# Where the first four gated tiles of an output projection are fetched and split, and where a shift state is transposed

## The chip, the cores and the metric

The kernel runs on one core of a Trainium2 chip. The time is the device time of one execution in microseconds; the median of three runs before the change is 1459.28 us (1458.47 to 1459.82). The engines are named as the profile names them: PE (matrix products), PEld (its weight loads), DVE (elementwise), ACT (activations, copies, casts), POOL (elementwise), and SP, which in this kernel issues the DMAs.

## What is computed

A trunk of two layers over 544 tokens (512 of a prompt and 32 of a sample), 1024 wide. Layer 0 mixes tokens with a recurrence (RWKV-7, 24 heads of 64), layer 1 with differential attention. Each layer also has a cross-attention over a memory of 256 rows with four heads. Both results are multiplied by a gate and go through one output projection:

```python
def rwkv_layer(x, mk, mv, prev_row, S0, norm_w, w_out, w_in, ...):
    h = rmsnorm(x, norm_w)
    p, qm, gate = jnp.split(h @ w_in, [RW_PROJ, RW_PROJ + MEM_W], axis=-1)
    y_mix, S_T, last_row = rwkv_mixer(p, prev_row, S0, ...)
    y_mem = mem_attention(qm, mk, mv)
    out = jnp.concatenate([y_mix, y_mem], axis=-1) * jax.nn.silu(gate)
    return x + out @ w_out, S_T, last_row
```

`S_T` (the recurrence's state) and `last_row` (the last projected row, "shift state", 37 x 128 values for the prompt and as many for the sample) are outputs too. Products of float32 are made of three passes with operands split in a high and a low part: `hh`/`hl` of the activations, `whi`/`wlo` of the weights.

## The kernel before

**Tiling.** Channels lie on the 128 partitions and the 544 tokens along the free axis, taken in two halves of 272. A projection to 128 channels is 8 tiles of the contracted dimension, three passes (`hh,whi`, `hl,whi`, `hh,wlo`) and two halves: 48 matmuls of 128x272 into a `ps_g` bank. `wlo` is made on DVE from the raw weights and their cast `whi` (ACT).

**Layer 0.** The 24 heads are worked in 12 pairs, numbered 0 to 11. Inside a pair a chain of chunks runs hop by hop: a product into `ps_c`, an evacuation by DVE (`avz`, or the new state `SB`) or ACT (`sv`, `yt`, `sd`), the next product. Between the hops the projections of later pairs fill PE, taken from a generator (`main`). The sequence is written out by hand: `PLAN` has 23 rows k with two halves each, `MPLAN` puts the steps of the memory attention at (row, head) of the pairs 10 and 11. While `ordered` is set, every engine and SP's queue issue in the order in which the program emits: an instruction at the head of a queue that waits holds back all that is behind it. Weight subtractions and gatings are put off in a list, `later`, and `some(room)` emits as many as a budget of DVE time allows; `spent` counts what the budget has used. `until` forces what a block needs, just before the block starts.

**What is gated.** `put` sends a gated tile (128 channels x 544 tokens: 12 of the heads, 0 to 11, and 4 of the memory attention, 12 to 15) to DRAM scratch, `oscr`. For the output projection `fetch` brings it back into a tile `lo`, and `gated` splits it: `hi` is the cast, on ACT; `lo` becomes the rest by a subtraction, on DVE for even tiles and on POOL for odd ones (line 1161).

**The end of layer 0.** After pair 11 the gate of head pair 11 (called gate 11 here) is projected, and pair 11's outputs are finished by `rw_finish` ("fin", "rsq" in `TAIL`), ending with `yt`, five transposes `ps_y` and the last gating. Between these steps `fill2` takes matmuls, first of gate 11, then of the output projection. Its units (`w_out`) are a block k of 128 output channels, a half of the gated tiles, and four tiles of it; the first two units use tiles 0 to 3. `ahead` splits one fetched tile and fetches another; NGATED is how many are fetched in advance.

**Shift state.** At the end of pair 9 two 37x128 transposes (`ps_sh`), one copy (`sho`) and two DMAs put it out, ahead of the memory attention's first loads (`cmt`, `mhk`, `mhv`, `cmv`) in the program.

Of the kernel before, what the change touches and what calls it, by code (L numbers as in the profile page):

```python
# [9 lines left out]
F32 = mybir.dt.float32  # L10
# [7 lines left out]
P = 128  # L18
# [7 lines left out]
NPAIR = MIXW // P  # L26
NMEM = 256
MH = 4
RW_PROJ = 3 * MIXW + 128
NPROJ = RW_PROJ // P  # L30
# [7 lines left out]
RAWS = 5  # L38
SGB = 2
HNB = 3  # L40
NGATED = 4
MADE = 6


# [2 lines left out]
LATER = 0.75  # L47
# [23 lines left out]
    [[("prep", 3, 0, 1.45), ("val", 1, 0.45, 0)], [("prep", 3, 0, 0.5)]],  # L71
    [[("out", 0, 1.6, 0.7)], [("prep", 3, 0, 0)]]]
MEMPE = 4.8
MPLAN = {10: [(0, 0), (1, 0), (2, 0), (3, 0), (4, 0), (5, 0), (6, 0), (6.5, 1), (7, 0), (8, 0), (9, 0), (10, 0), (10.5, 0), (12.5, 1),
# [9 lines left out]
OUT_ORDER = [0, 1, 2, 3, 4, 5, 6, 7, 8, 9, 10, 12, 13, 14, 15, 11]  # L84
# [21 lines left out]
class Trunk:  # L106
# [758 lines left out]
    def rw_outputs(self, st):  # L865
# [7 lines left out]
        yield  # L873
        self.state_out(self.SB[pr % 2][0], self.o[2][0, 0, 2 * pr : 2 * pr + 2])

    def state_out(self, S, dst):
        nc, p = self.nc, self.rk0
        ps = self.psm.tile([P, 4, P], F32, tag="m", name="ps_so")
        self.te.transpose(ps[:, 0, :], S[:], self.ident[:])
        so = p.tile([P, 64], F32, tag="so", name="so", bufs=1)  # L880
        for h in range(2):
            hc = slice(64 * h, 64 * h + 64)
            self.ae.copy(so[hc, :], ps[hc, 0, hc])
        self.se.dma_start(dst.rearrange("h v k -> (h v) k"), so[:])
# [30 lines left out]
        return self.o1[g] if self.o1 else sg  # L915

    def put(self, g, t):
        if not self.o1:
            self.se.dma_start(self.oscr[g // 8][:, g % 8, :], t[:])

# [249 lines left out]
    def w_out(self, i, p, order, consume, extra=None, o=None):  # L1170


        came, o = [], o or {}
        left = [g for g in order if g not in o]

        def fetch():
            if left:
                g = left.pop(0)
                came.append((g, self.fetch(p, g)))

        def ahead(n):
            for _ in range(n):
                if came:
                    g, t = came.pop(0)
                    o[g] = self.gated(g, *t)
                    fetch()

        for _ in range(NGATED):
            fetch()
        half = [[g for g in order if g // 8 == q] for q in range(2)]  # L1190
        units = [(k, q, half[q][4 * j : 4 * j + 4], j == 1) for q in range(2) for j in range(2) for k in range(2)]
        units += [(k, q, half[q], True) for k in range(2, KT) for q in range(2)]
        ws, ps = {}, {}
        halves = [slice(0, TH), slice(TH, T)]

        def products():
            for k, q, gs, last in units:
                if (k, q) not in ws:
                    ws[k, q] = self.weights(None, 0)
                hi, lo = ws[k, q]  # L1200
                ahead(len([g for g in gs if g not in o]))
                if q == 0 and k not in ps:
                    pool, tag = (self.psc, "c") if k == 1 else (self.psg, "g")
                    ps[k] = [pool.tile([P, 512], F32, tag=tag, name="ps_g") for _ in range(2)]
                end = q == 1 and last
                for vs in [halves] if k < 2 else [[v] for v in halves]:
                    for j, g in enumerate(gs):
                        if k < 2 and (j + k) % 2 == 0:
                            ahead(1)
                        if end and extra is not None and j == len(gs) // 2:  # L1210
                            extra(k, vs)
                        for v in vs:
                            out = ps[k][v.start // TH][:, :TH]
                            wh, wl = hi[:, g % 8, :], lo[:, g % 8, :]
                            for x, y in ((wh, o[g][0]), (wh, o[g][1]), (wl, o[g][0])):
                                self.te.matmul(out, x, y[:, v], start=q == 0 and g == half[0][0] and x is wh and y is o[g][0],
                                                 stop=end and g == gs[-1] and x is wl)
                                yield
                    if vs[-1].stop == T and last:
                        self.used()  # L1220
                    if end:
                        for v in vs:
                            consume(k, ps[k][v.start // TH][:, :TH], v)

        return products(), ahead
# [29 lines left out]
    def layer0(self, mem):  # L1255
        nc, o = self.nc, self.o
# [4 lines left out]
        mctx, rctx = ExitStack(), self.rctx  # L1261
        with ExitStack() as ctx:
# [66 lines left out]
                        yield from self.mem_block(i, kind, h, *hl(), wt, out, self.psm, "m")  # L1329
                    add(None, src, h * P, make)  # L1330

            mems = [{} for _ in range(MH)]
            rw_gate = lambda pr, j: add_gate(pr, sts[j], RW_PROJ + 512 + j * P, j % 2)
            mem_gate = lambda pr, h: add_gate(pr, mems[h], RW_PROJ + 512 + MIXW + h * P, h // 2)
            add_mems(0, 1, lambda: mem)
# [91 lines left out]
            for pr in range(NPAIR):  # L1427
                mplan = MPLAN.get(pr, ())
                took = [HOP + sum(us for x in y for kind, d, us, _ in x if 0 <= pr + d < NPAIR) for y in PLAN]
                load = [HOPV[k % 3] + sum(us for x in y for kind, d, _, us in x if 0 <= pr + d < NPAIR) for k, y in enumerate(PLAN)]  # L1430
                whole = sum(took) + MEMPE * len(mplan) / 12 + MAIN * each[pr]

                pace = [max(x, 1.4) for x in load] if each[pr] < 3 * 6 * KT else [1.0] * len(PLAN)
                due = [whole * sum(pace[:k]) / sum(pace) for k in range(len(PLAN) + 1)]
                room = (sum(load) + 2.3 * each[pr] / 48) / len(PLAN)
                t, left, spent = 0.0, each[pr], 0.0
                for k, y in enumerate(PLAN):
                    go("chain", pr)
                    t += HOP
                    spent += HOPV[k % 3]  # L1440
                    for half, x in enumerate(y):
                        for kind, d, us, vus in x:
                            if 0 <= pr + d < NPAIR and kind != "full":
                                go(kind, pr + d)
                                t += us
                                spent += vus
                        for at, h in mplan:
                            if at == k + half / 2:
                                if h not in mit:
                                    mit[h] = self.mem_steps(mems[h], 0, h, self.ma)  # L1450
                                    next(mit[h])
                                next(mit[h], None)
                                t += MEMPE / 12
                        if FULL not in x:
                            spent += self.some(room * (k + (half + 1) / 2) + 0.4 - spent)
                        while left and t + MAIN / 2 < (due[k + 1] if half else (due[k] + due[k + 1]) / 2):
                            next(main)
                            t += MAIN
                            left -= 1
                while left:  # L1460
                    next(main)
                    left -= 1
                if pr + 3 == NPAIR:
                    for _ in range(3):
                        go("prep", pr + 2)
                    while self.later:
                        self.later.pop(0)[0]()
                    ca.close()
                    self.ma = self.pool("mem0a", 1, ctx=ma, side="right")
                    ps = self.psm.tile([P, 512], F32, tag="m", name="ps_sh")  # L1470
                    so = self.ma.tile([NPROJ, 2, P], F32, name="sho")
                    for q in range(2):
                        self.te.transpose(ps[:NPROJ, q * P : q * P + P], self.shc[:, q, :], self.ident[:])
                    self.ae.copy(so[:], ps[:NPROJ, :256].rearrange("p (q c) -> p q c", q=2))
                    for q, n in ((0, 3), (1, 9)):
                        self.se.dma_start(o[n][0, 0].rearrange("(j p) -> j p", p=P), so[:, q, :])

            go("out", NPAIR - 1)
            fill(6)
# [7 lines left out]
        with ExitStack() as ctx:  # L1487
            p = self.pool("wo0", 1, ctx=ctx)
# [31 lines left out]

            rows(0)
            self.ahead = after[2:] + [(self.a[n][1], h * P) for n in ("w_mem_k", "w_mem_v") for h in range(MH)] + self.blocks1()
            wout, ahead = self.w_out(0, p, OUT_ORDER, consume, residual)

            def both():
                yield from main
# [27 lines left out]
            for i in range(5):  # L1554
                n = P if i < 4 else TS
# [259 lines left out]
    def run(self):  # L1815
# [3 lines left out]
        self.psm = self.pool("psm", 2, space=PS)  # L1819
        self.psx = self.pool("psx", 1, space=PS)  # L1820
        self.psc = self.pool("psc", 2, space=PS)
        self.mem = {}
        self.ordered, self.later, self.open = False, [], []
        self.place_no = self.acted = 0
        nc = self.nc
# [61 lines left out]
```

## Time and profile before

| | |
|---|---|
| median of 3 runs | 1459.28 us |
| span of the profiled execution | 1461.1 us |
| PE busy in it | 1403.8 us (96%) |
| DVE, ACT, POOL busy | 63%, 57%, 29% |
| PE waits from 600 to 626 us (start of pair 10) | 2.2 for `cmt`, 1.2 for `sv`, 0.5 and 0.2 for `yt` |
| PE waits from 626 to 706 us (pairs 10 and 11) | 0.4 to 0.9 each, for `mp`, `yt`, `sg`, `so` |
| PE waits from 706 to 760 us (start of the output projection) | 1.6 for `yt`, 1.3 for `lo` of DVE, 0.9 for `hi`, 0.5 for `lo` of POOL |

The profiled execution's time is its span, first instruction to last; it lies 1.8 us above the median of the runs, which were not profiled. A row of the timeline is a start in us, a duration in us, engine, line, operation, and `out<-in`; in square brackets stands how long the engine was idle before it and for whom. With xN, a row is N instructions in a row. Matmuls overlap, so that two neighbours start 0.125 us apart although each lasts 0.29. PEclk is the granted clock of PE, 1.00 at full speed.

### The profile page before, as it was taken

To read this page: it belongs to the slowest core of one execution; us is meant where nothing else is said; L and a number is where in the kernel's file an instruction comes from. 1 tells how busy PE (TensorE), PEld (TensorE's weight loads), DVE (VectorE), ACT (ScalarE), POOL (GpSimd) and SP (SyncE) were. 2 spreads that over 40 slices of the span, in tenths; PEclk is the share of its full clock that TensorE was granted. 3 is DMA by queue.
4 is the path that set the end of the run, shared out by engine and by line. 5 is a ranking of instruction groups with operands and counts; after the bars stand their busy time and mean duration, and the time that the engine had idled before them with its cause. 6 is when DMAs were issued, how large, how long until landed. Compare 5 with 4: busy or idle time off the path is not lost.

```text
span 1461.1 us, 32131 instructions
## 1 busy us (share of the span) xinstructions
PE 1403.8 (96%) x11978; PEld 1320.5 (90%) x11978; DVE 915.4 (63%) x2313; ACT 831.6 (57%) x2269; POOL 421.5 (29%) x868
## 2 busy tenths in 40 slices
PE   6998899999999999899899999999999999999997
PEld 5997899999999998798799998999989999899997
DVE  7565777787877877565733565664466745657533
ACT  6664667667677676565533365653466546565322
POOL 2025576566766557500210040100001002100200
PEclk9998999999999999999999999999999999999999
DMA  6442122332223222232554473232323222322321
GB/s 217 128 129 71 32 71 76 81 81 70 79 74 81 73 77 63 70 98 76 185 158 121 126 198 102 78 87 84 113 67 89 84 87 81 88 83 75 102 87 69
DMA packets 266534, 139.20 MB, mean 95 GB/s; under 512 B 57658, under 2 KB 256579, under 8 KB 266379
## 3 DMA queue, kind: packets, MB, share of 16 engines
q1 hardware_dynamic: 266378, 137.16, 33.1%
q8 instruction: 94, 1.54, 0.4%
q14 instruction: 62, 0.50, 0.1%
HBM read 110.98 MB, written 22.78 MB: 92 GB/s over the span
## 4 chain that ended last, share of the span: by engine, by line
PE 81%; DVE 8%; ACT 4%; issue 2%; DMA 2%; POOL 2%; SPq 1%; DVEq 0%; ACTq 0%; POOLq 0%
PE ps_g L103 56%; PE ps_c L103 4%; PE ps_s L103 3%; PE ps_o L103 2%; PE ps_at L103 2%; DVE wlo L103 1%; PE ps_v L103 1%; PE ps_mm L103 1%; SPq L103 1%; PE ps_mo L103 1%; POOL tm L721 1%; PE ps_ss L103 1%; PE ps_aT L103 1%; DVE pt L103 1%; PE ps_yc L103 1%
## 5 line engine op out<-in xcount | busy, mean ns | idle before, releaser
L103 PE MATMUL ps_g<-hh,wlo 128*128 128x272 f32 x1808 | 541.3, 299 | 1.4 <-DVE wlo L103 1.4
L103 PE MATMUL ps_g<-hh,whi 128*128 128x272 f32 x1808 | 540.1, 299 | 0.1
L103 PE MATMUL ps_g<-hl,whi 128*128 128x272 f32 x1808 | 535.6, 296 | 0.0
L103 DVE TENSOR_TENSOR wlo<-raw,whi 128x512 fp32r<-128x512 f32 x322 | 230.9, 728 | 205.6 <-ACT whi L103 196.2
L103 PEld LDWEIGHTS ps_g<-hh,wlo 128*128 128x128 f32 x1808 | 343.6, 190 | 6.4 <-DVE wlo L103 2.1
L103 PEld LDWEIGHTS ps_g<-hh,whi 128*128 128x128 f32 x1808 | 344.1, 190 | 4.4 <-PE ps_g L103 0.3
L103 PEld LDWEIGHTS ps_g<-hl,whi 128*128 128x128 f32 x1808 | 343.7, 190 | 3.6
L103 ACT CAST whi<-raw 128x512 fp32r<-128x512 f32 x322 | 194.7, 617 | 186.1 <-PE ps_g L103 132.6
L721 POOL TENSOR_TENSOR tm<-u,m 102x84 f32<-102x84 f32 (+23 forms) x372 | 158.3, 426 | 183.5 <-DMA m<-sc 155.4
L723 POOL TENSOR_TENSOR u<-u,tm 102x84 f32<-102x84 f32 (+23 forms) x372 | 158.5, 426 | 29.1
L103 PE MATMUL ps_g<-hi,whi 128*128 128x272 f32 x512 | 149.8, 292 | 0.9 <-ACT hi L103 0.9
L103 PE MATMUL ps_g<-lo,whi 128*128 128x272 f32 x512 | 148.4, 290 | 1.8 <-DVE lo L103 1.3
L103 PE MATMUL ps_g<-hi,wlo 128*128 128x272 f32 x512 | 148.3, 290 | 0.8 <-DVE wlo L103 0.8
L1706 POOL TENSOR_TENSOR kz<-k,kh 64x544 fp32r<-64x544 f32 x24 | 34.7, 1446 | 325.0 <-ACT kh L103 324.1
L103 PEld LDWEIGHTS ps_g<-lo,whi 128*128 128x128 f32 x512 | 96.9, 189 | 2.7 <-DVE lo L103 1.8
L103 PEld LDWEIGHTS ps_g<-hi,whi 128*128 128x128 f32 x512 | 97.0, 190 | 1.6 <-ACT hi L103 1.1
L103 PEld LDWEIGHTS ps_g<-hi,wlo 128*128 128x128 f32 x512 | 96.9, 189 | 1.1 <-DVE wlo L103 1.1
L103 DVE SCALAR_TENSOR_TENSOR SB<-ps_c,dl,sd 64x64 f32<-64x64 f32 x168 | 47.4, 282 | 49.0 <-PE ps_c L103 43.4
L103 ACT ACTIVATE pt<-ps_s,snm 128x128 f32<-128x128 f32 (+3 forms) x96 | 50.8, 530 | 23.8 <-DVE snm L103 23.0
L103 ACT COPY sv<-ps_c 64x64 f32<-64x64 f32 x192 | 39.5, 206 | 39.5 <-PE ps_c L103 37.7
L103 ACT ACTIVATE sg<-ps_g 128x272 f32<-128x272 f32 x64 | 25.3, 396 | 48.0 <-PE ps_g L103 45.5
L1161 POOL TENSOR_TENSOR lo<-og,hi 128x544 fp32r<-128x544 f32 x8 | 13.7, 1713 | 131.0 <-issue 130.5
(364 smaller groups left out, 2614.1 us busy)
## 6 DMA issues: line engine op xcount, KB each, us to landing
raw<-in_rw_in_dram SPq DMA_DIRECT2D x114, 256.0 KB
raw<-in_df_in_dram SPq DMA_DIRECT2D x112, 256.0 KB
raw<-in_w_out_dram SPq DMA_DIRECT2D x64, 256.0 KB
m<-sc SPq DMA_DIRECT2D x36, 128.0 KB
oscr<-sg SPq DMA_DIRECT2D x16, 272.0 KB
lo<-oscr SPq DMA_DIRECT2D x16, 272.0 KB
raw<-in_w_mem_k_dram SPq DMA_DIRECT2D x16, 256.0 KB
raw<-in_w_mem_v_dram SPq DMA_DIRECT2D x16, 256.0 KB
```

What stands on the lines that cost most here:

```text
L103: return lambda *a, **k: self.trunk.tie(self, issue(*a, **k))
L721: nc.gpsimd.tensor_tensor(tm[:, :n, :wd], u3[:, :n, kx : kx + 1].to_broadcast(sh), m3[:, kx : kx + 1, kx + 1 :].to_broadcast(sh), ALU.mult)
L723: nc.gpsimd.tensor_tensor(u3[:, :n, kx + 1 :], u3[:, :n, kx + 1 :], tm[:, :n, :wd], ALU.add)
L1161: (self.nc.gpsimd if g % 2 else self.ve).tensor_tensor(lo[:], t, hi[:].bitcast(F32), ALU.subtract)
L1706: nc.gpsimd.tensor_tensor(kz[rows[m], m, :], k[rows[m], :], hi.bitcast(F32), ALU.subtract)
```

## The change

Four things move; no arithmetic is added or left out.

1. Tiles 0 to 3 are fetched in pair 11 at row 0, into a new pool `wo0e`, and split there at the second halves of rows 7, 10, 13 and 16. Each split adds `LATER` = 0.75 us to `spent`. `w_out` gets them ready made.
2. In layer 0 eight tiles are fetched in advance in place of four (only tiles already put), and `ahead` fetches before it splits.
3. The shift state is transposed once (74x128), copied and put out in pair 10 at row 13, not at the end of pair 9.
4. In `MPLAN` the steps of head 0 in pair 10 move: (1, 0) goes, (10.5, 0) becomes (11, 0) and (11.5, 0).

```diff
-NGATED = 4
+NGATED = 8
...
-MPLAN = {10: [(0, 0), (1, 0), (2, 0), (3, 0), (4, 0), (5, 0), (6, 0), (6.5, 1), (7, 0), (8, 0), (9, 0), (10, 0), (10.5, 0), (12.5, 1),
+SHIFTED, SPLIT = 13, (7, 10, 13, 16)
+MPLAN = {10: [(0, 0), (2, 0), (3, 0), (4, 0), (5, 0), (6, 0), (6.5, 1), (7, 0), (8, 0), (9, 0), (10, 0), (11, 0), (11.5, 0), (12.5, 1),
...
+    def shift_out(self):
+
+        ps = self.psm.tile([P, 512], F32, tag="m", name="ps_sh")
+        so = self.ma.tile([2 * NPROJ, P], F32, name="sho")
+        self.te.transpose(ps[: 2 * NPROJ, :P], self.shc[:].rearrange("p q j -> p (q j)"), self.ident[:])
+        self.ae.copy(so[:], ps[: 2 * NPROJ, :P])
+        for q, n in ((0, 3), (1, 9)):
+            self.se.dma_start(self.o[n][0, 0].rearrange("(j p) -> j p", p=P), so[q * NPROJ : q * NPROJ + NPROJ, :])
...
     def put(self, g, t):
+        self.out.add(g)
         if not self.o1:
...
-        def fetch():
-            if left:
+        def fetch(n=1):
+            while left and len(came) < n and (self.o1 or left[0] in self.out):
                 g = left.pop(0)
                 came.append((g, self.fetch(p, g)))
 
         def ahead(n):
             for _ in range(n):
+                fetch()
                 if came:
                     g, t = came.pop(0)
                     o[g] = self.gated(g, *t)
-                    fetch()
-
-        for _ in range(NGATED):
-            fetch()
+                    fetch(depth)
+
+        depth = 4 if self.o1 else NGATED
+        fetch(depth)
...
+                        if half and pr == NPAIR - 2 and k == SHIFTED:
+                            self.shift_out()
+                        if half and pr == NPAIR - 1:
+                            if k == 0:
+                                came = [(g, self.fetch(early, g)) for g in OUT_ORDER[:4]]
+                            if k in SPLIT:
+                                g, tiles = came.pop(0)
+                                made[g] = self.gated(g, *tiles)
+                                spent += LATER
                         if FULL not in x:
                             spent += self.some(room * (k + (half + 1) / 2) + 0.4 - spent)
...
                     ca.close()
+                    early = self.pool("wo0e", 1, ctx=mctx, side="right")
                     self.ma = self.pool("mem0a", 1, ctx=ma, side="right")
-                    ps = self.psm.tile([P, 512], F32, tag="m", name="ps_sh")
-                    so = self.ma.tile([NPROJ, 2, P], F32, name="sho")
-                    for q in range(2):
-                        self.te.transpose(ps[:NPROJ, q * P : q * P + P], self.shc[:, q, :], self.ident[:])
-                    self.ae.copy(so[:], ps[:NPROJ, :256].rearrange("p (q c) -> p q c", q=2))
-                    for q, n in ((0, 3), (1, 9)):
-                        self.se.dma_start(o[n][0, 0].rearrange("(j p) -> j p", p=P), so[:, q, :])
...
-            wout, ahead = self.w_out(0, p, OUT_ORDER, consume, residual)
+            wout, ahead = self.w_out(0, p, OUT_ORDER, consume, residual, made)
```

At the start of pair 10, SP's queue before (`oscr_340<-sg_83` is the store of the last gated tile ahead of it, `cmt` the cached memory keys of head 0):

```order
L103 DMA out_dram<-so 128x64
L103 DMA oscr_340<-sg_83 128x544
L103 DMA out_dram<-sho 37x128 x2
L103 DMA cmt<-in_cache_mem_k_dram 128x2x128
L103 DMA mhk<-mkv_354 128x256
```

and with the change:

```order
L104 DMA out_dram<-so 128x64
L104 DMA oscr_340<-sg_83 128x544
L104 DMA cmt<-in_cache_mem_k_dram 128x2x128
L104 DMA mhk<-mkv_354 128x256
L104 DMA mhv<-mkv_878 128x256
```

The two stores of `sho` no longer stand ahead of `cmt`; they follow 22 rows later, at row 13 of the pair. On PE, the transposes of `cmt` (`ps_ck`) moved too, from right behind a hop (`ps_c<-sv,bt`) to behind 14 more matmuls of `ps_g` and the next hop (`ps_c<-SB`).

DVE in pair 11 around row 13, before (`mnm` is a maximum of the memory attention, `avz` the evacuation that the chain's next product waits for, `mp` a softmax):

```order
L103 SCALAR_TENSOR_TENSOR SB_576<-ps_c,dl,sd 64x64 x2
L103 TENSOR_REDUCE mnm<-ps_mm 128x2
L103 TENSOR_TENSOR avz<-ps_c,avz 64x128
L103 RECIPROCAL mrs<-mrs 128x2
L103 TENSOR_TENSOR mp<-mp,mrs 128x512
```

and with the change:

```order
L104 SCALAR_TENSOR_TENSOR SB_576<-ps_c,dl,sd 64x64 x2
L104 TENSOR_REDUCE mnm<-ps_mm 128x2
L104 TENSOR_TENSOR lo_9997<-lo_9997,hi_9996 128x544
L104 TENSOR_TENSOR avz<-ps_c,avz 64x128
L104 RECIPROCAL mrs<-mrs 128x2
L104 TENSOR_TENSOR mp<-mp,mrs 128x512
```

The subtraction for tile 2 stands ahead of `avz`; that for tile 0 stands likewise ahead of the `avz` at row 7. The cast `hi_9996` that it needs stands on ACT behind a softmax, a `whi` and the square `gsq`.

DVE at the end of pair 11 and at gate 11, before (`yt_102<-ps_yc` takes the chain's last outputs, `sg_84` is a gate):

```order
L103 SCALAR_TENSOR_TENSOR SB_576<-ps_c,dl,sd 64x64 x2
L103 TENSOR_TENSOR wlo<-raw,whi 128x512
L103 SCALAR_TENSOR_TENSOR bv_1777<-ps_y,PA,bv_1777 128x512
L103 SCALAR_TENSOR_TENSOR bv_1777<-ps_y,PA,bv_1777 128x32
L103 TENSOR_TENSOR avz<-ps_c,avz 64x128
L103 TENSOR_TENSOR wlo<-raw,whi 128x512
L103 SCALAR_TENSOR_TENSOR sg_83<-sg_83,bv_1777 128x544
L103 SCALAR_TENSOR_TENSOR sg_84<-sg_84,ps_g 128x272
L103 SCALAR_TENSOR_TENSOR SB_575<-ps_c,dl,sd 64x64 x2
L103 TENSOR_TENSOR yt_102<-ps_yc,yt_102 128x512
L103 SCALAR_TENSOR_TENSOR sg_84<-sg_84,ps_g 128x272
```

and with the change:

```order
L104 SCALAR_TENSOR_TENSOR SB_576<-ps_c,dl,sd 64x64 x2
L104 SCALAR_TENSOR_TENSOR bv_1777<-ps_y,PA,bv_1777 128x512
L104 SCALAR_TENSOR_TENSOR bv_1777<-ps_y,PA,bv_1777 128x32
L104 TENSOR_TENSOR avz<-ps_c,avz 64x128
L104 SCALAR_TENSOR_TENSOR sg_83<-sg_83,bv_1777 128x544
L104 SCALAR_TENSOR_TENSOR SB_575<-ps_c,dl,sd 64x64 x2
L104 TENSOR_TENSOR yt_102<-ps_yc,yt_102 128x512
L104 TENSOR_TENSOR wlo<-raw,whi 128x512 x2
L104 SCALAR_TENSOR_TENSOR sg_84<-sg_84,ps_g 128x272 x2
```

The two `wlo` of gate 11's weights and a gating of `sg_84` went behind `yt_102<-ps_yc`.

More of the change, by code (lines that the diff above doesn't have):

```diff
@@ L1330, in add_mems @@
                     add(None, src, h * P, make)
-            mems = [{} for _ in range(MH)]
+            mems, made = [{} for _ in range(MH)], {}
             rw_gate = lambda pr, j: add_gate(pr, sts[j], RW_PROJ + 512 + j * P, j % 2)
@@ L1821, in run @@
         self.psc = self.pool("psc", 2, space=PS)
-        self.mem = {}
+        self.mem, self.out = {}, set()
         self.ordered, self.later, self.open = False, [], []
```

## The prediction

> **What bounds the kernel now.** I read the page first: PE's share of the span, then of the chain that ended last.
>
> ```profile
> span 1461.1 us, 32131 instructions
> PE 1403.8 (96%) x11978; PEld 1320.5 (90%) x11978; DVE 915.4 (63%) x2313; ACT 831.6 (57%) x2269; POOL 421.5 (29%) x868
> PE 81%; DVE 8%; ACT 4%; issue 2%; DMA 2%; POOL 2%; SPq 1%; DVEq 0%; ACTq 0%; POOLq 0%
> ```
>
> PE is the bound, and the change leaves it its matmuls (two transposes become one). So only two things can change the time: PE's waits, and the clock at which it runs. The table of windows (columns: stretch, its length, then busy time of PE, PEld, DVE, ACT, POOL, then PEclk, DMA share, GB/s) shows where there are any near the change.
>
> ```profile
> 600.00:620.00 20.00, 16.20 (x177) 14.43 (x175) 6.96 (x18) 10.29 (x31) 13.99 (x43) 0.91 0.24 72
> 680.00:700.00 20.00, 18.77 (x130) 16.77 (x131) 14.05 (x41) 10.23 (x34) 0.00 (x0) 1.00 0.24 69
> 715.00:720.00 5.00, 2.67 (x15) 1.80 (x14) 4.73 (x12) 3.90 (x8) 1.48 (x2) 1.00 1.02 323
> 720.00:725.00 5.00, 3.02 (x17) 2.59 (x18) 3.49 (x3) 1.10 (x2) 3.15 (x2) 0.91 1.09 341
> 725.00:730.00 5.00, 5.00 (x33) 5.00 (x33) 3.98 (x5) 3.88 (x6) 3.17 (x2) 0.75 0.43 164
> ```
>
> Two places lose: the start of pair 10 (600 to 620: 3.8 us idle, clock 0.91) and the start of the output projection (715 to 725: 4.3 us idle, then clock 0.75). Pair 11 (680 to 700) loses 1.2 us in small waits; it is there that the change puts its new work.
>
> **Start of pair 10.** PE, then ACT and SP, from the timeline:
>
> ```profile
> 604.25 0.60 PE L103 MATMUL ps_bt<-ident,bk 128*128 128x128 f32 x4
> 606.01 0.41 PE L103 MATMUL ps_sh<-ident,shc 128*37 128x128 f32 x2 [1.16 <-ACT sv L103]
> 608.25 0.28 PE L103 MATMUL ps_g<-hh,wlo 128*128 128x272 f32 x1
> 608.37 0.29 PE L103 MATMUL ps_g<-hh,whi 128*128 128x272 f32 x1
> 611.06 0.41 PE L103 MATMUL ps_ck<-ident,cmt 128*128 128x128 f32 x2 [2.19 <-DMA cmt<-in_cache_mem_k_dram]
> 611.23 0.42 PE L103 MATMUL ps_g<-hl,whi 128*128 128x272 f32 x1
> 613.48 0.43 PE L103 MATMUL ps_g<-hh,wlo 128*128 128x272 f32 x1
> 615.15 0.48 PE L103 MATMUL ps_g<-hh,whi 128*128 128x272 f32 x1
> 618.45 0.49 PE L103 MATMUL ps_c<-sv,bt 128*128 128x128 f32 x2 [0.46 <-ACT yt L103]
> 605.98 0.59 ACT L103 COPY bt<-ps_bt 128x512 f32<-128x512 f32 x1
> 601.03 0.34 SPq L103 DMA_DIRECT2D oscr<-sg  x1
> 606.90 0.63 SPq L103 DMA_DIRECT2D out_dram<-sho  x2
> 607.64 0.41 SPq L103 DMA_DIRECT2D cmt<-in_cache_mem_k_dram  x1
> ```
>
> PE waits 2.19 us for `cmt`, issued only at 607.64 because the two stores of `sho` stand ahead of it on SP and wait for ACT's copy. Without them `cmt` follows the store of 601.03, so about 601.4, and it took 611.06 - 607.64 = 3.4 us to be used: there by 604.8, and `ps_ck` is now behind 14 more matmuls besides. The wait of 2.19 goes, and nothing that I find in the new order takes its place: the next loads on SP (`mhk` and so on) come six microseconds earlier too. Then the clock: the matmuls from 611.23 to 613.48 start 2.25 / 10 = 0.225 us apart, those at 608.25 and 608.37 0.12 apart. Eleven of them lose 1.1 us; the rest until 615.15 (1.67 us, a hop and four scores) loses at the same ratio 0.45 of its time, which is 0.75, or 0.5 if the hop's own latency stays. I take 1.6. The wait of 0.46 for `yt` at 618.45 goes too, as head 0's steps move ACT's work to later rows, but there a copy that stands ahead of another `yt` makes a new one of about 0.3: 0.2 to gain. The `ps_sh` pair cost nothing at its place, since the products behind it need `bt`, which ends at 605.98 + 0.59 = 606.57 anyway; at its new place one transpose costs 0.1. Sum: 2.19 + 1.6 + 0.2 - 0.1 = **3.9 gained** (2.2, the bare wait, to 4.8, with the whole wait for `yt` and 0.5 more for the clock).
>
> The clock needs a reason. In the row, a wait of 2.19 us that followed one of 1.16 by some three microseconds was enough to halve it for four. The Trainium skill ("TensorE: Matmul & The Clock Gate", Part 1) has the half clock come after one idle window of some 3.4 us and go after as much sustained work. By that rule neither wait alone would do it here, and the trace differs: it fell after less. With the change a wait of 606.57 - 604.85 = 1.7 (behind the last matmul's end, ahead of the 28 `ps_v`) with a hop in it is what is left there, and I take it as too little; if it is not, 1.6 of the 3.9 stay away (a rival below).
>
> **The splits in pair 11.** First the prices of a split, as it stands alone before: on ACT 0.64, on DVE 0.72, on POOL 1.35; then the rows at 676 and at 690 us between which the new ones fall.
>
> ```profile
> 715.46 0.64 ACT L103 CAST hi<-lo 128x544 fp32r<-128x544 f32 x1 [2.00 <-DMA lo<-oscr]
> 716.36 0.72 DVE L103 TENSOR_TENSOR lo<-lo,hi 128x544 fp32r<-128x544 f32 x1
> 717.01 1.35 POOL L1161 TENSOR_TENSOR lo<-lo,hi 128x544 fp32r<-128x544 f32 x1 [99.73 <-ACT hi L103]
> 676.23 0.61 ACT L103 CAST whi<-raw 128x512 fp32r<-128x512 f32 x1
> 676.90 0.27 DVE L103 TENSOR_TENSOR avz<-ps_c,avz 64x128 f32<-64x128 f32 x1
> 677.56 0.38 PE L103 MATMUL ps_c<-avz,at 128*128 128x128 f32 x2
> 685.96 0.48 ACT L103 ACTIVATE mp<-ps_mm,mnm 128x256 f32<-128x256 f32 x1 [4.83 <-DVE mnm L103]
> 691.66 0.75 ACT L103 ACTIVATE gsq<-yt 128x640 f32<-128x640 f32 x1
> 690.99 0.28 DVE L103 TENSOR_TENSOR avz<-ps_c,avz 64x128 f32<-64x128 f32 x1 [0.79 <-PE ps_c L103]
> 692.04 0.38 PE L103 MATMUL ps_c<-avz,at 128*128 128x128 f32 x2
> 694.73 0.70 PE L103 MATMUL ps_mm<-cmk,mq 128*128 128x256 f32 x2 [0.39 <-ACT so L103]
> ```
>
> (1) Tile 0: its cast stands behind the `whi` of 676.23, so it runs 676.84 to 677.48; the subtraction, ahead of `avz` on DVE, until 678.20; `avz` until 678.5. PE wanted it at 677.56: a wait of **0.95**. Behind the waiting subtraction stand `avz` and a `wlo`; the latter has room.
> (2) Tile 1: ACT is idle for 4.8 us before 685.96, and POOL for 99.7 before its row above, so in the whole pair: nothing. Were that cover gone, it would be up to a cast, 0.64.
> (3) Tile 2: its cast comes behind `gsq`, which ends at 692.41, so it ends at 693.05, the subtraction at 693.75, `avz` at 694.0 instead of 691.27. PE wanted it at 692.04: 1.95. The wait of 0.39 at 694.73 for `so`, copied on ACT meanwhile, goes in it: **1.55** net.
> (4) Tile 3: the cast lies behind a softmax whose turn has slack; POOL's subtraction beside DVE's small operations: 0 to 0.9, near tile 2's row I take **0.2**.
> (5) `spent` grows by 3 us, so two `wlo` go behind `yt<-ps_yc`. The row of the first, and those it now meets (the second stood 1.75 us later):
>
> ```profile
> 701.08 0.69 DVE L103 TENSOR_TENSOR wlo<-raw,whi 128x512 fp32r<-128x512 f32 x1
> 706.84 0.69 DVE L103 TENSOR_TENSOR yt<-ps_yc,yt 128x512 f32<-128x512 f32 x1 [0.43 <-PE ps_yc L103]
> 707.14 0.29 PE L103 MATMUL ps_g<-hh,wlo 128*128 128x272 f32 x1
> ```
>
> `yt` ends at 707.53, the first `wlo` at 708.2; gate 11's third matmul, at 707.14 before, needs it: **1.05** (0.8 to 1.3). The second is ready 0.6 later, behind twelve matmuls' time.
> The four fetches at row 0 are four issues on SP (0.45 us each by their row below, 2.74 / 6), 1.8 us ahead of weights that ACT casts 10 us later: hidden.
>
> Sum of the splits: 0.95 + 1.55 + 0.2 + 1.05 = **3.75 lost** (1.9, if half of it overlaps, to 5.5).
>
> **Start of the output projection.**
>
> ```profile
> 712.37 2.74 SPq L103 DMA_DIRECT2D lo<-oscr  x6
> 716.15 0.39 PE L103 MATMUL ps_g<-hi,whi 128*128 128x272 f32 x1 [0.92 <-ACT hi L103]
> 720.49 1.46 DVE L103 TENSOR_TENSOR lo<-lo,hi 128x544 fp32r<-128x544 f32 x1 [0.34 <-ACT hi L103]
> 721.87 1.96 DVE L103 TENSOR_TENSOR yt<-yt,q 128x640 f32<-128x640 f32 x1
> 723.88 1.21 PE L103 MATMUL ps_y<-ident,yt 128*128 128x128 f32 x5 [1.57 <-DVE yt L103]
> ```
>
> Before, 24 matmuls on tiles 0 to 3 run between waits for `hi` and `lo`, and `ps_y` waits for `yt` until 723.88. Now the 24 have their tiles and run in one piece, but that alone gains nothing: PE then stands until `yt`. `yt` is what counts, and ahead of it on DVE stand two subtractions (tiles 4 and 6) where there were three. Without the one at 720.49 `yt` starts at about 720.1, and lasts 0.8 alone or 1.96 as here, beside POOL's subtraction (the subtraction at 720.49 lasts twice its 0.72 likewise). `ps_y` comes at 721.0 to 722.1: **2.3 gained**, the middle (1.8 to 2.9). The wait is then one of about 3 us instead of six small ones; the half clock behind it (725 to 730 at 0.75) is in the time already and stays. Ten fetches, not six, now stand ahead of the next weights, which are wanted three units later: hidden, and if not, 1.8 us of issue.
>
> **The sum.** -3.9 - 2.3 + 3.75 = -2.45 against the profiled execution, 1461.1 to 1458.65. That execution lies 1.8 above the median of the runs, 1459.28; the same difference gives 1456.8. What a measurement of this kernel can tell from no change is about 0.2%, 2.9 us, so a bound at 1456.36: the forecast lies just above it.
>
> **The rivals.** (B) The splits hide better: the chain has slack at rows that I hold for tight, and half of 3.75 stays: -4.3, 1455.0. For it speaks that each later hop could catch up; against it that PE has only 1.2 us of waits in 680 to 700 to give. (C) The clock at the start of pair 10 does not recover, as 1.7 us of waiting stay: -0.85, 1458.4. (D) `yt` gains nothing, since `hi` of tile 6 lands later behind ten fetches: -0.15, 1459.1. (E) The other side: the clock is touchy. If waits of 1 to 2 us near each other halve it (2.19 behind 1.16 did), then the new ones at 677.6 and 692.0 and at gate 11 each bring four microseconds at half speed, 1.6 each, and pair 10's 1.6 is not won: -2.45 + 4.8 + 1.6 = +4, 1463.2. It decides from two such spells on. For it: the row of 611.06. Against it: 680 to 700 has 1.2 us of waits and a PEclk of 1.00. That the change doesn't do what it says I exclude: the order shows each move.
>
> **How the numbers follow.** Forecast 45% (its own range 1454.5 to 1458.8, by 1 us of error in each of its three sums), B 22%, C 10%, D 6%, E 17%. Faster by over 0.2%: 24 of the forecast's 45, all of B: 46%. Slower by over 0.2%: 14 of E's 17, 14%. The rest, 40%, within. The range 1452.9 (B with the upper ends of the gains) to 1461.3 leaves out 6% below and 13% above, most of E.
>
> **What would show it.** Pair 10 right: no wait for `cmt`, 0.125 us between matmuls at 611 to 615, and 600 to 620 some 4 us shorter. Pair 11 right: `ps_c` waits for DVE's `avz` near 677 and 692 by 1 and 2 us, a `ps_g<-hh,wlo` waits about 1 us at gate 11. Tail right: one wait, for `yt`, of 3 us, with 24 matmuls of `hi` and `lo` without a gap ahead of it. Wrong would be: PEclk under 1.00 in 660 to 710; `ps_y` still 9 us behind gate 11's last matmul; a wait for `raw` or `whi` anew.

## The result, and the profile after

The change made the kernel slower: 1463.6 us median (1461.01 to 1466.38, 19 runs) against 1459.1 (1455.24 to 1462.16, 19 runs), a ratio of 1.0030 with an interval of 1.0022 to 1.0038, about 4.4 us. Repeated beside other runs (experiment 11) the ratio was 1.0021 (1.0010 to 1.0032), about 3 us. Forecast were -2.45 us and a range up to 1461.3.

What follows is read from one profiled execution of each kernel, and executions of one kernel lie up to 7 us apart: those of the changed kernel took 1466.2 and, in experiment 11, 1465.4 us, both at the upper end of its runs. Device times lie about 1.7 us above the spans here (1.66 to 2.44 over all runs), so by this estimate the profiled execution before took about 1463 us, some 3.5 above the median and not 1.8; the forecast, a difference, is not changed by it.

The page, then the table of windows of the kernel after (columns as before; PEclk is the third number from the end):

```profile
span 1463.9 us, 32138 instructions
PE 1402.2 (96%) x11977; PEld 1319.4 (90%) x11977; DVE 916.7 (63%) x2313; ACT 830.0 (57%) x2269; POOL 421.3 (29%) x868
...
600.00:620.00 20.00, 18.38 (x184) 17.30 (x184) 10.01 (x25) 13.37 (x44) 15.24 (x43) 1.00 0.39 112
660.00:680.00 20.00, 17.44 (x122) 16.47 (x121) 11.71 (x29) 11.61 (x40) 0.00 (x0) 0.91 0.33 99
680.00:700.00 20.00, 17.42 (x119) 15.45 (x118) 13.20 (x32) 11.21 (x36) 2.69 (x2) 1.00 0.24 69
715.00:720.00 5.00, 5.00 (x42) 5.00 (x42) 4.45 (x16) 3.02 (x7) 0.67 (x1) 1.00 0.96 298
720.00:725.00 5.00, 0.64 (x6) 0.42 (x4) 5.00 (x4) 4.71 (x8) 3.83 (x3) 0.96 1.02 369
725.00:730.00 5.00, 4.45 (x20) 4.45 (x21) 4.96 (x7) 0.65 (x1) 1.67 (x1) 0.50 0.78 221
```

PE has as much work as before. Pair 10's start is repaired (18.4 busy of 20 at full clock, 16.2 at 0.91 before). Pair 11 now has a clock of 0.91 in 660 to 680, and 720 to 725 holds almost no work. The waits of PE, from 660 to 706 and from 706 to 760, say for whom (columns: us in total, times, longest):

```profile
PE ps_c L104 <- DVE avz L104: 2.4, 2, 1.7
PE ps_si L104 <- DMA SS<-in_state_rwkv_dram: 1.3, 1, 1.3
PE ps_y L104 <- DVE yt L104: 1.2, 1, 1.2
...
PE ps_y L104 <- DVE yt L104: 4.9, 1, 4.9
PE ps_g L104 <- DVE wlo L104: 0.9, 1, 0.9
```

To see where the time went, the starts of the same matmuls in the two timelines are set beside each other. What the last column gains or loses from row to row was gained or lost between these two places.

| matmul | before | after | difference |
|---|---|---|---|
| `ps_bt`, start of pair 10 | 604.25 | 603.10 | -1.15 |
| `ps_yc`, end of pair 10 | 656.97 | 651.71 | -5.26 |
| `ps_c<-SB,zr` behind the SS wait, pair 11 | 675.68 | 673.47 | -2.21 |
| `ps_c<-avz,at` behind tile 0's split | 677.56 | 676.19 | -1.37 |
| `ps_c<-avz,at` behind tile 2's split | 692.04 | 692.56 | +0.52 |
| `ps_mm`, the wait for `so` gone | 694.73 | 694.77 | +0.04 |
| `ps_y` of pair 10, behind tile 3's split | 700.61 | 701.87 | +1.26 |
| gate 11's third matmul | 707.14 | 709.43 | +2.29 |
| gate 11's last matmul | 714.95 | 717.34 | +2.39 |
| `ps_y` of pair 11 | 723.88 | 725.55 | +1.67 |
| 20th matmul behind it | 728.43 | 730.99 | +2.56 |
| end of the span | 1461.1 | 1463.9 | +2.8 |

The first 1.15 lie ahead of the change, in code that is the same in both: one execution against another. From pair 10 on the change lost 1.15 + 2.8 = 3.95 us in these two executions: 4.1 gained in pair 10, 3.05 lost up to the third row, 0.84, 1.9, 1.2 and 1.1 lost where pair 11 and gate 11 have their four new waits (0.5 got back at `so`), 0.7 gained at the tail's `yt` and 1.1 lost behind it. The tail is here what follows gate 11's last matmul.

**The first loss** stands where the forecast had put "hidden". SP and PE of the kernel after:

```profile
656.00 1.87 SPq L104 DMA_DIRECT2D lo<-oscr  x4
657.91 0.98 SPq L104 DMA_DIRECT2D raw<-in_rw_in_dram  x2
658.94 1.15 SPq L104 DMA_DIRECT2D SS<-in_state_rwkv_dram  x2
665.41 0.30 PE L104 MATMUL ps_si<-ident,SS 128*128 128x128 f32 x1 [1.33 <-DMA SS<-in_state_rwkv_dram]
667.40 0.63 PE L104 MATMUL ps_c<-SB,zr 128*128 128x128 f32 x2
...
660.00:665.00 5.00, 3.53 (x26) 3.10 (x24) 3.66 (x8) 2.78 (x10) 0.00 (x0) 1.00 0.93 278
665.00:670.00 5.00, 4.59 (x22) 4.52 (x23) 2.14 (x5) 1.31 (x6) 0.00 (x0) 0.66 0.04 11
```

`SS`, pair 11's initial state of the sample, is issued at 658.94 and used only at 665.41, 6.5 us later, through five microseconds in which the DMA engines are busy at 0.93 with 1.1 MB of tiles (4 x 272 KB) and 0.5 MB of weights. Before, with the tiles not there, it was issued 6.9 us ahead of its use at 669.2, with the DMA engines at 0.56, and nothing waited:

```profile
662.34 1.14 SPq L103 DMA_DIRECT2D SS<-in_state_rwkv_dram  x2
660.00:665.00 5.00, 4.89 (x59) 4.58 (x58) 1.54 (x5) 2.46 (x6) 0.00 (x0) 1.00 0.56 166
```

Now PE waits 1.33 us, and behind the wait the granted clock is 0.66; the two together make the 3.05.

**The other new waits** of pair 11 and gate 11 (PE, then the DVE and POOL rows that explain the third):

```profile
676.19 0.49 PE L104 MATMUL ps_c<-avz,at 128*128 128x128 f32 x2 [0.68 <-DVE avz L104]
692.56 0.49 PE L104 MATMUL ps_c<-avz,at 128*128 128x128 f32 x2 [1.74 <-DVE avz L104]
701.87 0.77 PE L104 MATMUL ps_y<-ident,yt 128*128 128x128 f32 x5 [1.20 <-DVE yt L104]
709.43 0.40 PE L104 MATMUL ps_g<-hh,wlo 128*128 128x272 f32 x1 [0.88 <-DVE wlo L104]
698.11 1.22 DVE L104 SCALAR_TENSOR_TENSOR nt<-q 128x20 f32<-128x20 f32 x1
699.36 0.18 DVE L104 TENSOR_TENSOR nt<-nt,q 128x20 f32<-128x20 f32 x1
697.95 1.35 POOL L1172 TENSOR_TENSOR lo<-lo,hi 128x544 fp32r<-128x544 f32 x1 [16.23 <-ACT hi L104]
```

A DVE operation on 20 columns that takes 0.18 us lasts 1.22 and ends at 699.33, with POOL's subtraction, which ends at 699.30.

**The tail**, in the same way:

```profile
720.22 5.50 ACT L104 CAST hi<-lo 128x544 fp32r<-128x544 f32 x8
719.81 2.04 DVE L104 TENSOR_TENSOR wlo<-raw,whi 128x512 fp32r<-128x512 f32 x2
721.77 1.85 DVE L104 TENSOR_TENSOR lo<-lo,hi 128x544 fp32r<-128x544 f32 x1
723.54 1.95 DVE L104 TENSOR_TENSOR yt<-yt,q 128x640 f32<-128x640 f32 x1
721.68 3.13 POOL L1172 TENSOR_TENSOR lo<-lo,hi 128x544 fp32r<-128x544 f32 x2 [0.99 <-ACT hi L104]
725.55 1.33 PE L104 MATMUL ps_y<-ident,yt 128*128 128x128 f32 x5 [4.91 <-DVE yt L104]
```

The 24 matmuls of tiles 0 to 3 run in one piece, as forecast. But the eight prefetched tiles are cast in one go, POOL works beside DVE almost without a break, and the last DVE operations ahead of `ps_y` are drawn out: 2.04 for two `wlo` that take 1.29 alone, 1.85 for a subtraction that takes 0.72, 1.95 for a `yt` that takes 0.82.

The second profile of the same kernel (experiment 11) differs in one of them. There the subtraction began just ahead of POOL's, not just behind it, and took 0.71; the wait was 4.0:

```profile
721.51 0.71 DVE L104 TENSOR_TENSOR lo<-lo,hi 128x544 fp32r<-128x544 f32 x1
722.14 1.95 DVE L104 TENSOR_TENSOR yt<-yt,q 128x640 f32<-128x640 f32 x1
721.52 5.57 POOL L1172 TENSOR_TENSOR lo<-lo,hi 128x544 fp32r<-128x544 f32 x3 [1.08 <-ACT hi L104]
724.15 1.33 PE L104 MATMUL ps_y<-ident,yt 128*128 128x128 f32 x5 [4.00 <-DVE yt L104]
```

### The profile page after: what moved, and what is told of

It is laid out like the page before. It is cut to its first block, busy times and chain, and to the rows that moved or that the text cites. A ratio compares the mean times of both kernels' runs of the same rounds, so it can differ in the third digit from the quotient of the medians.

```text
span 1463.9 us, 32138 instructions
## 1 busy us (share of the span) xinstructions
PE 1402.2 (96%) x11977; PEld 1319.4 (90%) x11977; DVE 916.7 (63%) x2313; ACT 830.0 (57%) x2269; POOL 421.3 (29%) x868
## 4 chain that ended last, share of the span: by engine, by line
PE 82%; DVE 8%; ACT 4%; DMA 2%; issue 2%; SPq 1%; DVEq 0%; ACTq 0%
PE ps_g L104 57%; PE ps_c L104 4%; PE ps_s L104 3%; PE ps_o L104 2%; PE ps_at L104 2%; PE ps_v L104 2%; DVE wlo L104 1%; SPq L104 1%; PE ps_mo L104 1%; PE ps_w L104 1%; PE ps_mm L104 1%; PE ps_aT L104 1%; DVE pt L104 1%; PE ps_yc L104 1%; PE ps_ss L104 1%
```

## The experiments

Each was timed in up to five rounds against the kernel before on the same chip. "The changed kernel" is at 1.0030 and 1.0021 of it. In the expectations e1_pair10 to e7_spent are experiments 1 to 7, and e9_dve, e10_taildve, e11_rows and e12_again are 8 to 11. Waits and clocks are of one profiled execution each.

**1. Pair 10's part alone**: the kernel before, with

```diff
+                        if half and pr == NPAIR - 2 and k == SHIFTED:
+                            self.shift_out()
...
-                    ps = self.psm.tile([P, 512], F32, tag="m", name="ps_sh")
...
-MPLAN = {10: [(0, 0), (1, 0), (2, 0), ... (10, 0), (10.5, 0), (12.5, 1),
+MPLAN = {10: [(0, 0), (2, 0), ... (10, 0), (11, 0), (11.5, 0), (12.5, 1),
```

> The kernel before with the pair 10 part of the change alone: shift state transposed at row 13, head 0's steps moved, no early fetches, four fetched ahead. Theory A (the ledger read from the two traces): the start of pair 10 gives its 4.1 us and nothing in it hurts later, so about 4 us under the kernel before, 1455, with 600 to 620 at PEclk 1.00 and no wait for cmt. Theory B (the gain at pair 10 is given back by a later wait whatever the splits do): within 1 us of the kernel before.

1457.62 us, ratio 0.9981 (0.9972 to 0.9991): 2.8 us faster (1.3 to 4.1). 600 to 620 has 18.47 us of PE's work at a clock of 1.00, and no wait for `cmt`. Theory A holds, its 4 at the edge of the interval; B, that the gain is given back somewhere, falls. So the rest of the change costs what is between 0.9981 and 1.0030 or 1.0021, 6 to 7 us.

**2. The four fetches behind the loads of SS and of head 3's keys:**

```diff
-                            if k == 0:
+                            if k == 4:
                                 came = [(g, self.fetch(early, g)) for g in OUT_ORDER[:4]]
```

> The changed kernel with the four early fetches issued behind the loads of SS and of head 3's memory keys (row 4 in place of row 0). Theory A: the bytes of the four fetches made SS late; its wait of 1.3 us and the 1.7 us at half clock behind it go, about 3 us under the changed kernel, 1460.5. Theory C (SS is late through something else, and the clock falls from the small waits of pair 11 in any case): less than 1 us gained, a wait of about 1 us at ps_si or PEclk below 1.00 in 660 to 680.

Ratio 1.0014 (1.0005 to 1.0023), 2.3 us less than the changed kernel's 1.0030 and 1.0 less than its 1.0021, where about 3 were expected. The wait for `SS` is gone from the list, and the window (660 to 680) is back at full clock:

```profile
660.00:680.00 20.00, 18.35 (x133) 16.42 (x131) 12.69 (x32) 11.94 (x40) 1.33 (x1) 1.00 0.33 105
```

Theory A holds for the wait: the four fetches' place on the queue made `SS` late, since moving them, and nothing else, took the wait away. What that is worth in time is less sure, as the intervals overlap: the 3 us include a spell at half clock that not every execution has (experiment 11).

**3. No splits among the finishing steps of pair 11:**

```diff
-                if kind == "split":
-                    ahead(1)
-                else:
+                if kind != "split":
                     go(kind, NPAIR - 1)
```

> The changed kernel with the splits between the finishing steps of pair 11 left to the output projection's own order (the entries 'split' of TAIL do no split). Theory A: yt stood behind two subtractions and ran beside POOL's, each of which doubled; one subtraction less ahead of it and fewer on POOL let yt start 2 us earlier and the wait of 4.9 us for yt falls to about 2 to 3, the half clock behind it shortens: 2 to 3.5 us under the changed kernel. Theory D (yt waits for the chain of its own small operations and for the two wlo, so the splits cost nothing): wait for yt unchanged within 0.5 us.

Ratio 1.0004 (0.9996 to 1.0013), 3.8 us under 1.0030 and 2.5 under 1.0021. The wait for `yt` at the tail falls from 4.9 (4.0 in experiment 11) to 2.3, and 720 to 730 runs at full clock:

```profile
720.00:725.00 5.00, 2.70 (x22) 2.49 (x21) 4.21 (x5) 2.44 (x4) 4.80 (x3) 1.00 1.09 337
725.00:730.00 5.00, 5.00 (x43) 5.00 (x41) 1.99 (x4) 0.81 (x2) 0.00 (x0) 1.00 0.97 321
```

Theory A holds; D falls. Ahead of `yt` now stands one subtraction in place of two, and the two `wlo` before it take 1.29 in place of 2.04, as POOL starts later; `yt` itself still takes 1.95 beside POOL. Of the remedies tried one at a time this one gained the most by its ratio.

**4. Tile 3 split at row 10, not 16:**

```diff
-SHIFTED, SPLIT = 13, (7, 10, 13, 16)
+SHIFTED, SPLIT = 13, {7: (0,), 10: (1, 3), 13: (2,)}
...
```

> The changed kernel with tile 3 split at row 10, right behind tile 1, and not at row 16. Theory A: POOL's subtraction of tile 3 at row 16 held DVE's small operations of the inverse root (one of 0.18 us took 1.22 and ended when POOL's did), so ps_y's wait of 1.2 us goes: 1.2 us under the changed kernel. Theory E (DVE is late by its own queue, and POOL has no part in it): the wait of 1.2 us stays, and the small operation takes 0.18 us in either.

The wait of 1.2 us for `yt` is not in the list of 660 to 706 any more, and the small operation takes 0.18; theory A holds. The ratio, 1.0016 (1.0006 to 1.0026), is 2 us under 1.0030 but less than 1 under 1.0021, so the time agrees and does not settle it.

**5. All four tiles at row 10**, with the fetches of experiment 2 (`SPLIT = {10: (0, 1, 2, 3)}`):

> e2_late with all four tiles split at row 10, where ACT is idle for 4.3 us in the changed kernel, in place of rows 7, 10, 13 and 16. Theory A: the waits of PE for avz (0.7 and 1.7) and for yt (1.2) came from where the splits stand, so they go, 3.4 us under e2_late less 0.5 for waits of the old kernel that come back: about 1459 if e2_late is 1462. Theory F (pair 11 is full, any place costs as much): less than 1 us under e2_late, new waits of DVE's avz or sg near row 10.

Ratio 1.0003 (0.9994 to 1.0013), 1.6 us under experiment 2, half of what was expected, with intervals that overlap. The waits for `avz` and `yt` went, but there is a new one; the list of 660 to 760 begins:

```profile
PE ps_y L104 <- DVE yt L104: 3.8, 1, 3.8
PE ps_mm L104 <- DVE sg L104: 1.7, 1, 1.7
```

The wait for `sg` was 0.4. At row 10 two subtractions stand ahead of `sg` on DVE and POOL's two run beside it. Theory A is right on the cause and F on the place: not free, but cheaper.

**6. The lot** (experiments 1 to 5 together, and `spent` not raised):

> Everything that the runs so far speak for: pair 10's part, the fetches behind SS, all four splits at row 10, no 'split' entries done in TAIL, and spent not raised. Theory A: pair 10's 4 us stay, pair 11 costs nothing, the tail's wait for yt is about 2.5 us with no half clock behind it in place of 5.4 us of waits and 1.5 of clock: 4 + 3.5 = 7 us under the kernel before on the same chip, under e1_pair10 by 3. Theory F: no better than e1_pair10.

1454.79 us (5 runs), ratio 0.9964 (0.9951 to 0.9977): 5.3 us faster than before and 2.5 under experiment 1's ratio. That is less than the 7 expected, and two things of theory A did not come: pair 11 costs something, since the wait of 1.7 at row 10 stays with a PEclk of 0.92 in 680 to 700 behind it; and behind the tail's wait for `yt`, 2.3, PEclk is 0.73 in 715 to 720, where none of the half clock was to be left. F is not excluded by the times alone: the intervals of experiments 1 and 6 just overlap.

**7. `spent` not raised, all else as in the change:**

```diff
-                                spent += LATER
```

> The changed kernel without raising spent for the splits, all else as it is. Theory A: the two wlo return ahead of yt<-ps_yc and gate 11's third matmul no longer waits 0.9 us: 1.0 us under the changed kernel, so about 1462 to 1463 where the changed kernel has 1464 to 1465. Theory G (the budget was needed: without it DVE is late for the hops or for yt in pair 11): the wait for wlo goes but those for avz or yt grow by as much.

Ratio 1.0022 (1.0012 to 1.0032). The wait of 0.9 for `wlo` at gate 11 is gone, but PE then waits the longer at the tail, 6.3 in place of 4.9 (4.0 in experiment 11):

```profile
717.13 2.01 DVE L104 TENSOR_TENSOR wlo<-raw,whi 128x512 fp32r<-128x512 f32 x2 [1.41 <-ACT whi L104]
719.07 1.85 DVE L104 TENSOR_TENSOR lo<-lo,hi 128x544 fp32r<-128x544 f32 x1
720.84 1.96 DVE L104 TENSOR_TENSOR yt<-yt,q 128x640 f32<-128x640 f32 x1
```

The cost at gate 11 was real and hardly worth anything: with the tail as it is, `yt` is set by DVE's queue, and PE arriving earlier only waits. Here DVE waits for the cast `whi`, which stands on ACT behind a tile's cast that waited 1.50 us for its fetch. Neither theory had this.

**8. No subtraction of layer 0 on POOL:**

```diff
-        (self.nc.gpsimd if g % 2 else self.ve).tensor_tensor(lo[:], t, ...)
+        (self.nc.gpsimd if g % 2 and self.o1 else self.ve).tensor_tensor(lo[:], t, ...)
```

> The changed kernel with every subtraction of a gated tile of layer 0 on DVE, none on POOL. Theory A (DVE and POOL hold each other up): beside no POOL work, the two wlo ahead of yt take 1.3 us in place of 2.0, each subtraction 0.7 in place of 1.85, yt 0.8 in place of 1.95, the small operation of pair 11 0.18 in place of 1.22; with two subtractions more ahead of yt, yt ends 1.5 to 2 us earlier, and the wait of 4.9 falls to about 3. Theory D (the durations are the instructions' own): they stay, and the wait grows by the two subtractions, to 6 or more.

Ratio 1.0012 (1.0003 to 1.0020). DVE of this kernel, in pair 11 and at the tail:

```profile
697.39 0.18 DVE L104 SCALAR_TENSOR_TENSOR nt<-q 128x20 f32<-128x20 f32 x1
718.67 1.29 DVE L104 TENSOR_TENSOR wlo<-raw,whi 128x512 fp32r<-128x512 f32 x2
719.87 1.35 DVE L104 TENSOR_TENSOR lo<-lo,hi 128x544 fp32r<-128x544 f32 x2
721.14 0.82 DVE L104 TENSOR_TENSOR yt<-yt,q 128x640 f32<-128x640 f32 x1
```

All durations are back at what they are alone: 0.18, 1.29, 0.7 each, 0.82. Though DVE now has four subtractions ahead of `yt` and not two, PE's wait falls from 4.9 (4.0 in experiment 11) to 3.1, and `ps_y` starts 6.4 us behind gate 11's last matmul, not 8.2 (7.3). Theory A holds, and this is the case that tells it: more work on DVE, and it is done sooner. It is not free in pair 11, where tile 3's subtraction, now ahead of `avz` on DVE, makes a third wait for `avz` of 0.9 and leaves one for `yt` of 0.6; and PEclk still falls to 0.68 in 720 to 725.

**9. Experiment 6 with the tail's subtractions on DVE** (`g % 2 and (self.o1 or g < 4)`):

> e6_best with the tail's subtractions on DVE (tiles 4 to 15), POOL keeping tiles 1 and 3 at row 10. Theory A (POOL beside DVE doubles it): yt takes 0.8 in place of 1.96, the wait of 2.3 us for yt falls to about 1.2, 1 to 2 us under e6_best (the clock included). Theory H (DVE fills up with the eight more subtractions, and a later wlo or tile is late): new waits of PE for lo or wlo after 720, no gain over e6_best.

1453.54 us, ratio 0.9955 (0.9938 to 0.9972). The tail's wait falls from 2.3 to 1.2 with no slow clock behind it; H falls, no wait for `lo` or `wlo` comes. The gain over experiment 6, 0.9 of a thousandth, is inside the intervals.

**10. The casts of the four tiles together at row 10, the subtractions spread:**

```diff
+                            if k == 10:
+                                for g, (hi, lo, tv) in came:
+                                    self.ae.copy(hi[:], tv)
+                                    made[g] = hi, lo
+                            for g in SPLIT.get(k, ()):
+                                hi, lo, tv = dict(came)[g]
+                                (self.nc.gpsimd if g == 1 else self.ve).tensor_tensor(lo[:], tv, ...)
...
+SHIFTED, SPLIT = 13, {10: (0, 1), 11: (2,), 14: (3,)}
```

> e10_taildve with the four casts left together at row 10, where ACT is idle, but the subtractions spread: tile 0 on DVE and tile 1 on POOL at row 10, tile 2 on DVE at row 11, tile 3 on DVE at row 14. Theory A: the wait of 1.7 us at row 10 for sg came from two subtractions ahead of it and POOL beside it, so it falls to 0.5 or less, 1.2 us under e10_taildve. Theory F (any place costs as much): a wait of about 1 us for avz, yt or mp elsewhere.

1450.84 us (1449.06 to 1451.77, 6 runs) against 1459.28, ratio 0.9939 (0.9924 to 0.9953): 8.9 us faster than the kernel before, 12 faster than the change in the same rounds. PE's waits from 660 to 760 in this kernel are all there is:

```profile
PE ps_y L104 <- DVE yt L104: 1.2, 1, 1.2
PE ps_c L104 <- ACT yt L104: 0.9, 2, 0.6
PE ps_mm L104 <- DVE sg L104: 0.4, 1, 0.4
PE ps_mm L104 <- ACT so L104: 0.4, 1, 0.4
```

Theory A holds: the wait for `sg` is 0.4 again, and none came in its place. With the casts and subtractions in gaps of their engines, the tail's kept off POOL and no splits among the finishing steps, the early tiles and pair 10 together are worth 9 us; pair 10 alone was worth 2.8.

**11. The changed kernel once more:**

> The changed kernel once more, unchanged, beside these. Theory A: slower than the kernel before by about 4 us again, with a wait of about 1 us for SS; whether PEclk falls behind that wait, as in its first profile (0.66 from 665 to 670), is open: e3_tail, e4_tile3, e7_spent and e9_dve had the wait of 0.8 to 1.1 us with PEclk at 1.00, so I expect 1.00 with 0.6 probability.

Ratio 1.0021 (1.0010 to 1.0032), 3.1 us slower where about 4 were expected. The wait for `SS` is there, 1.2 us, and the clock fell behind it again, against my 0.6:

```profile
665.00:670.00 5.00, 5.00 (x27) 4.64 (x26) 2.14 (x5) 1.74 (x7) 0.00 (x0) 0.66 0.01 4
```

In experiments 3, 4, 7 and 8, where the fetches also stand at row 0, the wait was 0.8 to 1.1 and PEclk 1.00: the spell was in two of the six profiles with this queue.

## Why the prediction was wrong, point by point

**Pair 10: right.** Forecast 3.9 gained (2.2 to 4.8), measured 4.1 between the first two rows of the table; alone it made the kernel 2.8 us faster (1.3 to 4.1), so less than the 3.9 by its time. The clock recovered, so rival C falls.

**The splits, tile 0, tile 2 and gate 11: right.** 0.95, 1.55 and 1.05 were forecast; the timelines give 0.84, 1.9 less 0.5, and 1.0. The in-order queues were followed correctly, cast by cast. But the sum took each as worth its time at the end, and in experiment 7 gate 11's was not: what is lost ahead of a wait that another engine sets can be given back there.

**The step that failed first: "the four fetches at row 0 ... 1.8 us ahead of weights that ACT casts 10 us later: hidden".** I asked what of SP's issue time was late, and only for the weights. Behind the fetches on the queue stood `SS` too, whose use had come 6.9 us after its issue. The four issues, 1.87 us of SP, left it 5.1, and with 1.1 MB more ahead of it it took 6.5. It measured 1.33 of wait and, with the clock, 3.05 us; with the fetches moved it was gone (experiment 2). Which of the two made it late, the later issue or the bytes, is not shown, since moving the fetches takes both away.

**Tile 3, a term mis-sized.** I took 0.2 out of 0 to 0.9; it was 1.2. I knew from 720.49 that DVE doubles beside POOL's subtraction, and did not apply it to operations of 0.18 us, where the factor is not two: the operation waits for the whole of POOL's. With POOL out of the way the operation took 0.18 again in experiments 4 and 8, and in experiment 4 the whole wait went.

**The tail, mis-sized, and the clock behind it.** Forecast were 2.3 gained (1.8 to 2.9). From gate 11's last matmul to `ps_y` it was 8.9 us before, 8.2 and 7.3 in the two profiles of the changed kernel, and 7.1 to 7.2 in experiments 2, 4 and 5, which have the same tail: 0.7, 1.6 and 1.8 gained. The step "without the one at 720.49 `yt` starts at about 720.1" gave tile 6's subtraction its 0.72 of before. That held in the second profile (0.71) and not in the first, where it began 0.09 us behind POOL's and took 1.85; `yt` was at its slow end, 1.95, in both. What failed in both is the clock: the 20 matmuls behind `ps_y` took 5.4 us in place of 4.55, so "the half clock behind it ... is in the time already and stays" did not hold. Up to the 20th of them the term was +0.2 in the first profile (+0.4 with the 0.24 up to the end of the span, as the sum below takes it), -0.8 in the second, and -1.9 in experiments 2, 4 and 5, where the 20 took 4.4 to 4.5. So its wrong sign is that of one execution, and its size was too large in all five. Experiments 3 and 9 show what helps: fewer splits or less POOL ahead of `yt`, a wait of 2.3 or 1.2, and a clock of 1.00 behind it.

**The rivals.** D (`yt` gains nothing) gave -0.15 and was nearest for the tail of the first profile, but through POOL and the clock; a tile that lands late shows ahead of `yt` in experiment 7 only. E's +4 is near the measured +4.4, in the main by luck: it had half clock behind the waits for `avz` and at gate 11 and none of pair 10's clock won, and the runs show 1.00 there (680 to 700, 705 to 710) and pair 10's clock back. The one spell in pair 11 came behind the wait for `SS`, which E did not have. B fell: the four costs in pair 11 and at gate 11 came out in full in the timelines.

In sum, the table's executions differ by +3.95, which is 6.4 above the forecast of -2.45: 3.05 for the fetches, 1.0 for tile 3 and 2.7 for the tail (from -2.3 to +0.4) are 6.8, less 0.4 by which the other terms came out better. The medians' +4.4 lies 6.9 above it, the repeat's +3.1 lies 5.5 above. How these divide over the terms is not shown: removed one at a time, they gained 1.0 to 2.3 (experiment 2), 0.7 to 2.0 (4), about 0 to 1.2 (7) and, for the tail, 2.5 to 3.8 (3), each against both ratios of the changed kernel, with intervals that mostly overlap.

## What to carry to other kernels

A prefetch is hidden only if everything behind it on the queue is early by the time that its issue and its bytes take, not only the loads that come to mind: go through the queue to the first load that somebody waits for. Put fill work on an engine in the place where its own operands are ready and the engine idles, part by part (casts here, subtractions there, as in experiment 10); done as one step, a subtraction that waits for its cast holds what stands behind it on DVE, here the chain's `avz`. Split work between DVE and POOL only where neither is on the path: at the tail the two together took longer than DVE alone (experiment 8). And take a second profile before explaining a difference of 1 us: here the same kernel's wait was 4.9 in one and 4.0 in the other.

## What the runs showed of the hardware

**DVE and POOL exclude each other for some operations.** A DVE operation of 0.18 us lasted 1.22, until POOL's subtraction ended; with POOL empty it was 0.18. At the tail it mattered who began: DVE's subtraction took 1.85 where POOL's began 0.09 us ahead of it (721.68 and 721.77), and 0.71 where its own began 0.01 us ahead (721.51 and 721.52). The Trainium skill ("SBUF — State Buffer", on who interferes with whom) has a DVE operation with two SBUF inputs and a GpSimd operation that reads SBUF block each other for the whole instruction, whichever comes first. These rows agree, and by that rule the 0.2 of the forecast would have been up to a POOL subtraction, 1.35.

**The half clock came behind waits shorter than I had thought.** A wait of 1.33 and one of 1.2 for `SS` were followed by 0.66 from 665 to 670 in two profiles of the changed kernel, while those of 0.8 to 1.1 at the same place in experiments 3, 4, 7 and 8 left it at 1.00. The Trainium skill ("TensorE: Matmul & The Clock Gate", Part 1) speaks of an idle window of some 3.4 us; no wait for `SS` was that long, so the rule as a length of one wait does not fit. Nor does a shorter length: behind the wait of 1.7 us for `sg` the clock of 680 to 700 was 0.92 and 0.93 in experiments 6 and 9 and 1.00 in experiment 5, and behind a wait of 2.3 at the tail it was 0.73 in experiment 6 (715 to 720) and 1.00 in experiment 3 (720 to 730). What else decides was not tried.
